# Low parts of the weights: all on VectorE while branch A is open, every second one on GpSimd elsewhere

## The chip, the cores and the metric

The kernel runs on one core of a Trainium2 chip. The metric is the device time of one execution in microseconds. TensorE (PE) multiplies matrices, VectorE (DVE), ScalarE (ACT) and GpSimd (POOL) work element by element, SyncE (SP) issues most of the transfers.

## What is computed

One step of a trunk of two layers, on 384 tokens (128 of a prompt, 256 of a latent grid) of width 2048. Each layer projects the modulated stream once, runs three mixers on the parts, and projects their outputs back:

```python
proj = jnp.matmul(u, lp['w_in']).astype(f32)
...
y_a, s_rwkv = rwkv_mixer(a_rkv, (a_wdf, a_wdb), (a_adf, a_adb), a_gate, lp, s_rwkv0)
y_b, mstate = mlstm_mixer(b_qk, b_v, b_o, b_i, b_f, b_gate, lp, mstate0)
y_c, kv_own = diff_attn_mixer(c_q, c_k, c_v, c_gate, lp, lam_init, ctx_kv)
mixed = jnp.concatenate([y_a, y_b, y_c], axis=-1).astype(x.dtype)
out = jnp.matmul(mixed, lp['w_out'])
x_new = layer_norm(DEEPNORM_ALPHA * x + gate[:, None] * out, lp['ln_g'], lp['ln_b'])
```

A is a recurrence with a 64x64 state per head in both directions, B a chunked matrix memory, C a differential attention.

## The kernel before

**Projections.** The two big projections are done in three products of fp32r numbers: the activations are kept as a high part `uh` and a low part `ul`, and so is each weight. A tile `raw` of weights comes by DMA in two halves of 128x512 (128x520 for B's values). `cut` splits a half: ScalarE copies it to `hi`, rounded to fp32r, and one subtraction, `raw - hi`, makes `lo`. A counter `ncut` gives every fourth subtraction to GpSimd (`CPOOL = 4`), the others to VectorE. There are four buffers each of `hi` and `lo`, and 688 halves in the program. PE then multiplies `uh,hi`, `ul,hi` and `uh,lo` into an `acc` tile: 12 matmuls for a usual half, 9024 in the program.

**The order.** One Python object, `Hybrid`, writes all instructions down in the order in which every engine will run them; each engine is a queue. The plan of a layer is a list of projection steps. The mixers are generators ("streams") that yield between short groups of instructions. Between projection steps `pump` lets streams go on whose inputs are ready by the planner's own clocks: `spend` adds to an engine's clock what `cost` says of an instruction, for VectorE 1.042 per element and 69, for GpSimd's two-input operations 2.1 per element and 149. `pump` returns when VectorE's or ScalarE's clock is more than `SLACK` ahead of PE's. Which engine gets a low part therefore goes into the order of everything behind it. No time on the chip goes into it.

**Branch A.** `a_start` spawns four streams: `AF` (`a_front`), `AD` (`a_blocks`), `AI` (`a_inverse`) and `A` (`a_scan`, with `a_end`). They pass 12 units (a chunk of 64 tokens in one direction) from one to the next; `AF` may be at most two units ahead of the scan. A unit's front begins with four `LP,lora` matmuls into a tile that becomes `th`; behind the last unit `AF` computes a bonus for each of four head pairs, with matmuls `big,const`. Branch A must be out of the tile `big0` before B's first projection is written there:

```python
def b_first(self):
    self.drain("AF")
    ...
    self.QK = self.mt([128, 8, T], "big0")
```

`drain` goes on with every stream that is ready, the one with the earliest clock first, until the named stream has ended; no projection step is written in that time. `b_first` stands in the plan ahead of B's first `q` step (`MIX`), behind 2304 projection matmuls of the program in layer 0 and 6816 in layer 1. A second `drain("A", "post")` follows at `to_b`, three steps later.

Of the kernel before, what the change touches and what calls it, by code (L numbers as in the profile page):

```python
# [14 lines left out]
AF = mybir.ActivationFunctionType  # L15
# [31 lines left out]
FILL = (4, 4, 4)  # L47
BLOCKS = (8, 4)
LAGP, LAGX = (100.0, 150.0), 0.0
CPOOL = 4  # L50
PESHARE = 2000.0, 2000.0
HEAD = ("PG", 2), ("QHt", 2), ("Tt", 2), ("BK", 1), ("QH", 1), ("UV", 1), ("ce00", 1), ("ce10", 1)
MIX = "cccqqqvvvvq", "cccqqqvvvvq"
# [148 lines left out]
class Hybrid:  # L202
# [212 lines left out]
    def execute(self, plan):  # L415
        data = [st for st in plan if st.kind != "c"]
        HB = KB // 2
        raws, halves = {}, {}
        issued = at = 0
        ring = RAWB + len(self.extra)  # L420
        early, taken, free = self.early, [], set()
        rooms = [i for i, st in enumerate(data) if st.room]

        def load(upto):
            nonlocal issued
            while issued < min(upto, len(data)):
                st, i = data[issued], issued
                if st.room:
                    k = rooms.index(i)
                    if k >= len(ROOMS) and rooms[k - len(ROOMS)] not in free:  # L430
                        return
                    tag, n, o = ROOMS[k % len(ROOMS)]
                    if o == 0:
                        self.room = self.mt([128, n], tag, bufs=2 if tag == "GE" else 1)
                    r = self.room[:, o:o + 1024]
                elif i < early and i % ring >= RAWB:
                    r = self.extra[i % ring - RAWB]
                elif len(taken) >= RAWB and taken[-RAWB] not in free:
                    return
                else:  # L440
                    taken.append(i)
                    r = self.keep("wp", self.wp.tile([128, KB * WMAX], F32, tag="raw", bufs=RAWB, name=self.nm("raw")), RAWB)
                k = st.parts * HB
                rv = r[:, 0:k * st.n].rearrange("p (k c) -> p k c", k=k)
                self.nc.sync.dma_start(rv, st.src())
                raws[i] = (r, rv, self.end)
                issued += 1

        def ahead(j):
            n = j + (ring if j < early else LOADS)  # L450
            load(n + sum(1 for i in rooms if j < i < n + len(ROOMS)))

        def cut(j, h):
            st = data[j]
            r, rv, t = raws[j]
            n = HB * st.n
            hi = self.keep("wp", self.wp.tile([128, HB * WMAX], F32R, tag="hi", bufs=CUTB, name=self.nm("hi")), CUTB)
            lo = self.keep("wp", self.wp.tile([128, HB * WMAX], F32R, tag="lo", bufs=CUTB, name=self.nm("lo")), CUTB)
            x = r[:, n * h:n * h + n]
            self.nc.scalar.copy(hi[:, 0:n], x)  # L460
            self.ncut = (self.ncut + 1) % CPOOL
            (self.nc.vector if self.ncut else self.nc.gpsimd).tensor_tensor(lo[:, 0:n], x, hi[:, 0:n].bitcast(F32), OP.subtract)
            if h == st.parts - 1:
                free.add(j)
            halves[j, h] = tuple(y[:, 0:n].rearrange("p (k c) -> p k c", k=HB) for y in (hi, lo)) + (self.end,)

        def front():

            k = (j, 1) if data[j].kind == "w" and now + 1 < data[j].parts else (j + 1, 0)
            if k in halves:  # L470
                return halves[k][2]
            return raws[k[0]][2] if k[0] in raws and data[k[0]].kind == "a" else 0.0

        self.more, self.front = lambda: cuts(j, now), front
        todo = [(j, h) for j, st in enumerate(data) if st.kind == "w" for h in range(st.parts)]

        def cuts(j, h):

            nonlocal at
            while at < len(todo) and todo[at] <= (j, h):  # L480
                cut(*todo[at])
                at += 1
            n = sum(1 for x in halves if x > (j, h))
            while at < len(todo) and n < CUTB - (1 if data[j].kind == "w" else 0) and todo[at][0] < issued:
                if raws[todo[at][0]][2] > self.clk["PE"] + AHEAD[self.l]:
                    break
                cut(*todo[at])
                at += 1
                n += 1
                ahead(j)  # L490

        j = now = self.ncut = 0
        ahead(0)
        for st in plan:
            if j == len(data):
                self.more, self.front = lambda: None, lambda: 0.0
            if st.kind == "c":
                st.fn()
                self.pump()
                continue  # L500
            ahead(j)
            if st.kind == "a":
                now = 1
                cuts(j, 1)
                r, rv, t = raws.pop(j)
                st.fn(rv)
            else:
                for h in range(st.parts):
                    now = h
                    cuts(j, h)  # L510
                    hv, lv, t = halves.pop((j, h))
                    st.fn(h, hv, lv)
                raws.pop(j)
            free.add(j)
            j, now = j + 1, 0
# [458 lines left out]
    def a_start(self):  # L974
        self.spawn(self.a_norm(), "N", lambda: self.have["k"] < 4)
        self.units, self.fronts, self.blocks = {}, {}, {}
        self.nf = self.nd = self.ni = self.ny = 0
        self.hold = False
        self.spawn(self.a_scan(), "A", lambda: self.have["v"] < 4 or (self.ny < 12 and self.ny >= self.ni))
        self.spawn(self.a_blocks(), "AD", lambda: self.nd < 12 and (self.nd >= self.nf or self.nd > self.ni))  # L980
        self.spawn(self.a_inverse(), "AI", lambda: self.ni < 12 and self.ni >= self.nd)
        self.spawn(self.a_front(), "AF", lambda: self.hold and self.nf - self.ny >= 2 or any(self.have[x] < n for x, n in (("n", 4), ("r", 4), ("lora", 2))))

    def a_lora(self, j, src):
        for d in range(2):
            o, i = self.LW[64 * j:64 * j + 64, d, :], src[64 * d:64 * d + 64]
            if j == 0:
                self.act(o, i, AF.Tanh)
            else:
                self.nc.scalar.copy(o, i)  # L990
        self.have["lora"] += 1
        yield
# [1100 lines left out]
```

## Time and profile before

| | before |
|---|---|
| median of 3 runs | 2233.82 us (2230.44 to 2238.89) |
| the profiled execution | 2234.41 us, of which the span 2232.7 us |
| PE busy | 2131.0 us, 95% |
| DVE busy | 1376.1 us, 62% |
| ACT busy | 950.1 us, 43% |
| POOL busy | 651.1 us, 29% |
| mean granted PE clock | 0.983 of full speed |

Busy time is the time in which an engine has at least one instruction under way. PE's matmuls overlap, so their own durations add up to more than its busy time, and one fp32 matmul can stand in the trace as two records. The line number of nearly all instructions is L155, the helper through which they are issued, so rows are told apart by their tiles: `mx` is a PSUM tile of the mixers, `acc` one of the projections, `mixed` holds A's working data (and the gates and outputs), `GE`, `QH`, `PG`, `Xo`, `Xd` and `th` are A's, `ce`, `cmx`, `cq` and `ck` are attention's.

### The profile page before, as it was taken

The numbers are of one execution on the slowest core, as the hardware profiler recorded it, in microseconds if no ns is written. First come the engines' busy times: TensorE is split into PE (matmuls) and PEld (weight loads), VectorE is DVE, ScalarE is ACT, GpSimd is POOL, SyncE is SP. The second block draws the span as 40 slices with busy tenths as digits, with TensorE's granted clock in tenths as the row PEclk, the third lists the DMA queues.
The fourth block names the chain that finished last, engine by engine and source line by source line (L and its number), as shares of the span: only waits on it lengthen the run. The fifth ranks groups of instructions, "written<-read, shape, count | busy, mean of one in ns | idle before, by whom it ended". The sixth has DMA issues, their size and how long they took to land. (4 is left out here: it accounts for less than half of the span.)

```text
span 2232.7 us, 44851 instructions
## 1 busy us (share of the span) xinstructions
PE 2131.0 (95%) x17261; PEld 1875.6 (84%) x17261; DVE 1376.1 (62%) x3704; ACT 950.1 (43%) x2215; POOL 651.1 (29%) x930
## 2 busy tenths in 40 slices
PE   6999999999999999999998999999999999999998
PEld 3778878778778788889997998787888789999997
DVE  2667766766675523578338677776776754367634
ACT  3345344353343533445326453444444354344543
POOL 3111433324332211111435223242343312111344
PEclk9999999999999999999998999999999999999998
DMA  9995433433434464554465442223232224333444
GB/s 323 317 320 148 135 112 110 128 100 108 148 99 137 151 194 155 171 154 152 153 198 185 137 123 91 78 76 105 70 93 79 78 83 152 114 114 118 141 146 144
DMA packets 313791, 314.83 MB, mean 141 GB/s; under 512 B 17569, under 2 KB 309030, under 8 KB 313450
## 3 DMA queue, kind: packets, MB, share of 16 engines
q1 hardware_dynamic: 305450, 299.49, 43.1%
q0 software_dynamic: 3616, 10.22, 1.4%
q8 instruction: 136, 2.23, 0.4%
q10 hardware_dynamic: 4512, 2.26, 0.4%
q14 instruction: 77, 0.63, 0.1%
HBM read 298.81 MB, written 13.12 MB: 140 GB/s over the span
## 5 line engine op out<-in xcount | busy, mean ns | idle before, releaser
L155 PE MATMUL acc<-uh,hi 128*128 128x384 f32 x2240 | 808.0, 361 | 11.6 <-ACT uh L155 7.7
L155 PE MATMUL acc<-uh,lo 128*128 128x384 f32 x2240 | 763.0, 341 | 5.8 <-POOL lo L155 3.4
L155 PE MATMUL acc<-ul,hi 128*128 128x384 f32 x2240 | 762.9, 341 | 1.3 <-DVE ul L155 1.3
L155 DVE TENSOR_TENSOR lo<-raw,hi 128x512 fp32r<-128x512 f32 (+1 forms) x496 | 361.8, 739 | 519.2 <-ACT hi L155 508.7
L155 ACT CAST hi<-raw 128x512 fp32r<-128x512 f32 (+1 forms) x659 | 395.7, 618 | 401.3 <-PE acc L155 259.4
L155 POOL TENSOR_TENSOR lo<-raw,hi 128x512 fp32r<-128x512 f32 (+1 forms) x163 | 221.9, 1361 | 927.3 <-ACT hi L155 860.0
L155 PEld LDWEIGHTS acc<-uh,hi 128*128 128x128 f32 x2240 | 426.6, 190 | 76.4 <-issue 35.8
L155 PEld LDWEIGHTS acc<-uh,lo 128*128 128x128 f32 x2240 | 425.3, 190 | 9.2 <-DVE lo L155 4.9
L155 PEld LDWEIGHTS acc<-ul,hi 128*128 128x128 f32 x2240 | 426.2, 190 | 6.0 <-DVE ul L155 3.1
L155 PE MATMUL acc<-hi,uh 128*128 128x256 f32 (+1 forms) x768 | 226.5, 295 | 2.8 <-ACT hi L155 1.1
L155 PE MATMUL acc<-lo,uh 128*128 128x256 f32 (+1 forms) x768 | 216.8, 282 | 1.0 <-DVE lo L155 1.0
L155 PE MATMUL acc<-hi,ul 128*128 128x256 f32 (+1 forms) x768 | 216.1, 281 | 0.0
L155 PEld LDWEIGHTS acc<-hi,uh 128*128 128x128 f32 x768 | 144.5, 188 | 20.3 <-issue 10.9
L155 PEld LDWEIGHTS acc<-lo,uh 128*128 128x128 f32 x768 | 144.6, 188 | 1.8 <-DVE lo L155 1.8
L155 PEld LDWEIGHTS acc<-hi,ul 128*128 128x128 f32 x768 | 144.7, 188 | 0.0
L155 ACT ACTIVATE ce<-mx,cmx 128x384 f32<-128x384 f32 (+1 forms) x96 | 48.0, 505 | 113.2 <-DVE cmx L155 110.1
L155 PE MATMUL ada<-raw,sil 128*32 128x256 f32 x1088 | 88.4, 399 | 1.8 <-DMA raw<-in_w_ada_dram 1.8
L155 ACT COPY mixed<-mx 64x256 f32<-64x256 f32 x120 | 44.0, 366 | 104.4 <-PE mx L155 102.7
L155 PEld LDWEIGHTS mx<-mixed 128*64 128x64 f32 x1536 | 53.5, 139 | 26.3 <-issue 11.1
L155 PE MATMUL mx<-mixed 128*64 128x64 f32 x1536 | 66.9, 230 | 3.3 <-DVE mixed L155 2.9
L155 DVE TENSOR_TENSOR mixed<-mx,mixed 128x256 f32<-128x256 f32 (+1 forms) x96 | 40.1, 418 | 30.1 <-PE mx L155 29.7
L155 DVE TENSOR_REDUCE cmx<-mx 128x1 f32<-128x384 f32 (+1 forms) x96 | 40.4, 460 | 19.8 <-PE mx L155 19.5
(435 smaller groups left out, 2940.5 us busy)
## 6 DMA issues: line engine op xcount, KB each, us to landing
raw<-in_w_in_dram SPq DMA_DIRECT2D x224, 512.0 KB
raw<-in_w_ada_dram SPq DMA_DIRECT2D x136, 512.0 KB
raw<-in_w_out_dram SPq DMA_DIRECT2D x64, 512.0 KB
big<-in_w_ada_dram SPq DMA_DIRECT2D x42, 512.0 KB
raw<-in_w_in_dram SPq DMA_DIRECT2D x32, 520.0 KB
GE<-in_w_ada_dram SPq DMA_DIRECT2D x14, 512.0 KB
cq<-xs SPq DMA_DIRECT2D x32, 192.0 KB
big<-in_w_in_dram SPq DMA_DIRECT2D x21, 256.0 KB
```

What stands on the lines that cost most here:

```text
L155: r = f(*args, **kw)
```

## The change

`CPOOL` becomes 2, and while one of A's four streams is open the counter is held at 1, which sends the low part to VectorE:

```diff
--- before.py
+++ after.py
@@ -47,7 +47,7 @@
 FILL = (4, 4, 4)
 BLOCKS = (8, 4)
 LAGP, LAGX = (100.0, 150.0), 0.0
-CPOOL = 4
+CPOOL = 2
 PESHARE = 2000.0, 2000.0
 HEAD = ("PG", 2), ("QHt", 2), ("Tt", 2), ("BK", 1), ("QH", 1), ("UV", 1), ("ce00", 1), ("ce10", 1)
 MIX = "cccqqqvvvvq", "cccqqqvvvvq"
@@ -458,7 +458,8 @@
             lo = self.keep("wp", self.wp.tile([128, HB * WMAX], F32R, tag="lo", bufs=CUTB, name=self.nm("lo")), CUTB)
             x = r[:, n * h:n * h + n]
             self.nc.scalar.copy(hi[:, 0:n], x)
-            self.ncut = (self.ncut + 1) % CPOOL
+
+            self.ncut = 1 if self.busy_a() else (self.ncut + 1) % CPOOL
             (self.nc.vector if self.ncut else self.nc.gpsimd).tensor_tensor(lo[:, 0:n], x, hi[:, 0:n].bitcast(F32), OP.subtract)
             if h == st.parts - 1:
                 free.add(j)
@@ -980,6 +981,9 @@
         self.spawn(self.a_blocks(), "AD", lambda: self.nd < 12 and (self.nd >= self.nf or self.nd > self.ni))
         self.spawn(self.a_inverse(), "AI", lambda: self.ni < 12 and self.ni >= self.nd)
         self.spawn(self.a_front(), "AF", lambda: self.hold and self.nf - self.ny >= 2 or any(self.have[x] < n for x, n in (("n", 4), ("r", 4), ("lora", 2))))
+
+    def busy_a(self):
+        return any(s.name in ("A", "AD", "AI", "AF") for s in self.streams)
 
     def a_lora(self, j, src):
         for d in range(2):
```

Of the 688 low parts GpSimd makes 172 in the program before and 189 in the changed one: while A is open 76 before and none now (36 and 40 in the two layers), elsewhere 96 before and 189 now. The instructions themselves, and those of PE, ACT and SP, are the same; their order changes where the planner's clocks lead to another choice.

On GpSimd, in layer 1 at the front of the twelfth and last unit of A (`GE`, `QH`, `ci` and `big` are its products, `th` a memset; `UV` and `Xd` belong to the scan and the inverse), there stands before:

```order
L155 COPY UV_20345<-big_2795_14457 64x256 x2
L155 TENSOR_TENSOR Xd_20159<-Xd_20159,own_20350 128x256
L155 MEMSET th_20381 128x4
L155 TENSOR_TENSOR lo_20398<-raw_20176,hi_20397 128x512
L155 TENSOR_TENSOR GE_20512<-th_20381,big_2793_14455 64x256
L155 TENSOR_TENSOR QH_20518<-q_3978_20384,BK_20377 64x4x2x64
L155 TENSOR_TENSOR ci_20521<-BK_20377,big_2793_14455 128x256
L155 TENSOR_TENSOR big_2793_14455<-ci_20521,Tt_14957 128x4x64
```

and in the changed program, at the same front:

```order
L155 COPY UV_20745<-big_2795_14457 64x256 x2
L155 TENSOR_TENSOR Xd_20548<-Xd_20548,own_20750 128x256
L155 TENSOR_TENSOR GE_20870<-th_20717,big_2793_14455 64x256
L155 TENSOR_TENSOR QH_20876<-q_4056_20720,BK_20713 64x4x2x64
L155 TENSOR_TENSOR ci_20879<-BK_20713,big_2793_14455 128x256
L155 TENSOR_TENSOR big_2793_14455<-ci_20879,Tt_15073 128x4x64
```

The subtraction `lo` is gone from between A's products; no other stands on GpSimd from A's opening to its end.

On PE, in layer 1, the bonus of A (`big,const`) stands before between projection matmuls, ahead of the place where `b_first` drains `AF`:

```order
L155 MATMUL mx_20691<-mixed_14454 64x64 x8
L155 MATMUL mx_20701<-big_2793_14455,const 128x384
L155 MATMUL acc_20654<-uh_125,hi_20531 128x384
L155 MATMUL acc_20654<-ul_126,hi_20531 128x384
L155 MATMUL acc_20654<-uh_125,lo_20532 128x384
L155 MATMUL acc_20655<-uh_125,hi_20531 128x384
L155 MATMUL acc_20655<-ul_126,hi_20531 128x384
L155 MATMUL acc_20655<-uh_125,lo_20532 128x384
L155 MATMUL mx_20710<-mixed_14454 64x64 x8
L155 MATMUL mx_20721<-big_2793_14455,const 128x384
L155 MATMUL mx_20724<-mixed_14454 64x64 x8
```

In the changed program the four bonus matmuls are the end of a row of instructions without any projection matmul (`cvc,ce` and `cvv,ce` are attention's), and the first matmul of the step behind `b_first` follows:

```order
L155 MATMUL mx_21009<-cvc_4023_20603,ce_4109_20913 128x128
L155 MATMUL mx_21009<-cvv_19762,ce_4109_20913 128x128 x2
L155 MATMUL mx_21015<-big_2793_14455,const 128x384
L155 MATMUL mx_21018<-mixed_14454 64x64 x8
L155 MATMUL mx_21067<-big_2793_14455,const 128x384
L155 MATMUL mx_21070<-mixed_14454 64x64 x8
L155 MATMUL mx_21081<-big_2793_14455,const 128x384
L155 MATMUL mx_21084<-mixed_14454 64x64 x8
L155 MATMUL mx_21107<-big_2793_14455,const 128x384
L155 MATMUL acc_21117<-uh_125,hi_20435 128x384
L155 MATMUL acc_21117<-ul_126,hi_20435 128x384
L155 MATMUL acc_21117<-uh_125,lo_20436 128x384
```

That row of instructions is what `drain("AF")` writes in layer 1. Before it wrote nothing there. It now holds 204 instructions on PE (170 matmuls and 34 transposes, 128 of them 64x64 matmuls), 109 on DVE (12 of them row maxima of attention, 7 shuffles), 57 on ACT and 43 on POOL, of A's units 10 to 12 and of the last two heads of C. The front of the twelfth unit begins in it:

```order
L155 MATMUL mx_20657<-LP_14459,lora_12739 128x128 x4
L155 MATMUL mx_20665<-const,ce_4029_20615 128x128
L155 MATMUL mx_20668<-mixed_14454 64x64 x8
L155 MATMUL mx_20678<-cvv_19762,ce_4020_20594 128x128
L155 MATMUL mx_20686<-cvv_19762,ce_4030_20617 128x128
L155 MATMUL mx_20690<-mixed_14454 64x64 x8
```

Before, that front stood 162 projection matmuls ahead of `b_first`. In layer 0 both programs have `AF` ended ahead of `b_first`; the drain writes nothing.

## Rows read from the trace of the kernel before

**Rows 1.** Page, part 1: busy time and share of each engine.

```profile
span 2232.7 us, 44851 instructions
PE 2131.0 (95%) x17261; PEld 1875.6 (84%) x17261; DVE 1376.1 (62%) x3704; ACT 950.1 (43%) x2215; POOL 651.1 (29%) x930
```

**Rows 2.** Windows, four stretches: busy us (records) by engine, clock, DMA.

```profile
core 0: us, PE busy (x) PEld busy (x) DVE busy (x) ACT busy (x) POOL busy (x), PEclk, DMA share, GB/s
230.00:760.00 530.00, 505.66 (x4949) 419.81 (x4947) 355.56 (x1054) 221.21 (x597) 169.31 (x279) 0.98 0.40 120
760.00:1290.00 530.00, 513.18 (x3360) 471.51 (x3353) 290.24 (x720) 223.22 (x464) 142.04 (x166) 0.99 0.53 165
1290.00:1790.00 500.00, 474.02 (x4653) 414.82 (x4652) 362.77 (x1029) 215.19 (x567) 175.78 (x283) 0.99 0.30 88
1790.00:2232.00 442.00, 429.88 (x2744) 406.78 (x2744) 236.32 (x610) 196.44 (x411) 116.35 (x133) 0.98 0.40 127
```

**Rows 3.** PE's waits (us, times, longest): 1290 to 1790 us, then 230 to 760.

```profile
PE mx L155 <- DVE mixed L155: 7.3, 7, 3.2
PE mx L155 <- DVE GE L155: 3.6, 5, 1.4
...
PE mx L155 <- DVE ce L155: 2.2, 2, 2.1
PE mx L155 <- DVE csm L155: 1.8, 1, 1.8
...
PE acc L155 <- DVE VC L155: 0.8, 1, 0.8
...
PE mx L155 <- DVE mixed L155: 6.8, 5, 2.7
PE mx L155 <- DVE GE L155: 3.6, 6, 1.5
...
PE mx L155 <- DVE mod L155: 3.2, 2, 1.7
...
PE acc L155 <- DVE lo L155: 1.5, 2, 1.2
```

**Rows 4.** Groups by shape (busy us, mean ns, idle before): low parts, whole span.

```profile
L155 DVE TENSOR_TENSOR lo<-raw,hi 128x512 fp32r<-128x512 f32 x448 | 329.0, 744 | 419.5 <-ACT hi L155 409.0 <-PE acc L155 5.4 <-PE mx L155 2.7
...
L155 POOL TENSOR_TENSOR lo<-raw,hi 128x512 fp32r<-128x512 f32 x147 | 201.0, 1367 | 791.2 <-ACT hi L155 723.8 <-PE mx L155 37.4 <-PE acc L155 10.9
```

**Rows 5.** Out-projection of layer 1: window, then GpSimd's sums (groups).

```profile
2100.00:2200.00 100.00, 100.00 (x572) 100.00 (x571) 36.88 (x64) 42.95 (x75) 46.76 (x40) 1.00 0.51 165
...
L155 POOL TENSOR_TENSOR ce<-ce,gt 128x384 f32<-128x384 f32 x26 | 37.3, 1436 | 0.3 <-ACT gt L155 0.3
...
L155 POOL TENSOR_TENSOR ce<-ce,mixed 128x384 f32<-128x384 f32 x26 | 26.4, 1016 | 0.1
```

**Rows 6.** Timeline of PE: start us, us, instructions, xcount.

```profile
1727.02 0.61 PE L155 MATMUL mx<-LP,lora 128*128 128x128 f32 x4
...
1767.00 0.81 PE L155 MATMUL mx<-big,const 128*128 128x384 f32 x2
...
1783.23 0.45 PE L155 MATMUL acc<-uh,hi 128*128 128x384 f32 x1
1783.51 0.34 PE L155 MATMUL acc<-ul,hi 128*128 128x384 f32 x1
1783.69 0.34 PE L155 MATMUL acc<-uh,lo 128*128 128x384 f32 x1
1783.87 0.34 PE L155 MATMUL acc<-uh,hi 128*128 128x384 f32 x1
```

**Rows 7.** Windows of one tile: mx, then lo in two stretches.

```profile
core 0: us, PE busy (x) PEld busy (x) DVE busy (x) ACT busy (x), PEclk, DMA share, GB/s
1290.00:1790.00 500.00, 175.41 (x2775) 136.68 (x2776) 86.36 (x208) 82.57 (x255) 0.99 0.30 88
...
core 0: us, PE busy (x) PEld busy (x) DVE busy (x) POOL busy (x), PEclk, DMA share, GB/s
1290.00:1790.00 500.00, 190.31 (x594) 112.49 (x594) 74.76 (x99) 45.85 (x33) 0.99 0.30 88
...
1790.00:2232.00 442.00, 236.08 (x730) 137.13 (x730) 87.41 (x123) 56.60 (x41) 0.98 0.40 127
```

**Rows 8.** Groups: attention's row maxima, LP,lora matmuls, activation of th.

```profile
L155 DVE TENSOR_REDUCE cmx<-mx 128x1 f32<-128x384 f32 (+1 forms) x96 | 40.4, 460 | 19.8 <-PE mx L155 19.5
...
L155 PE MATMUL mx<-LP,lora 128*128 128x128 f32 x192 | 26.6, 281 | 0.8 <-DVE GE L155 0.8
...
L155 ACT ACTIVATE th<-th 128x512 f32<-128x512 f32 x24 | 15.2, 632 | 54.4 <-DVE th L155 54.4
```

**Rows 9.** Windows at the layer boundary, columns as in rows 2.

```profile
1183.00:1193.00 10.00, 6.45 (x20) 5.53 (x21) 9.57 (x17) 6.59 (x14) 6.65 (x10) 0.53 0.51 172
1193.00:1204.00 11.00, 11.00 (x64) 10.74 (x63) 8.96 (x15) 9.50 (x21) 6.88 (x8) 1.00 0.44 145
```

**Rows 10.** Timeline: a low part on GpSimd and one on VectorE.

```profile
1344.87 1.30 POOL L155 TENSOR_TENSOR lo<-raw,hi 128x512 fp32r<-128x512 f32 x1 [1.18 <-ACT hi L155]
...
1345.35 1.37 DVE L155 TENSOR_TENSOR lo<-raw,hi 128x512 fp32r<-128x512 f32 x1 [1.88 <-ACT hi L155]
```

## The prediction

> **What bounds the kernel now.** I read the page first: of the span TensorE (PE) is busy 95%, VectorE (DVE) 62%, GpSimd (POOL) 29% [rows 1]. So the time is TensorE's work plus its idle time, 102 us, and an engine that only gets more or less busy changes nothing until TensorE waits for it. Then the stretches [rows 2]: branch A is open at about 230 to 760 us and 1290 to 1790 us, and there TensorE is idle for 24.3 and 26.0 us, with VectorE at 67% and 73%. In the other two stretches it is idle 16.8 and 12.1 us, much of that at the layer boundary and the end. Third, TensorE's waits in the two A stretches [rows 3]: small ones, mostly for branch A's own VectorE results (`mixed`, `GE`); for low parts little (VectorE's 1.5 us in layer 0, and none above 1 us in layer 1). So low parts are not what TensorE waits for. What they do is take time from an engine on which branch A's chain runs.
>
> **Low parts by themselves.** A low part takes 744 ns on VectorE and 1367 ns on GpSimd [rows 4]. In the order of the changed kernel the low parts of GpSimd go from 172 to 189, of 688: in the two A stretches from 76 to 0, elsewhere from 96 to 189. So VectorE gets 76 more in A, 57 us of work, 40 of them (30 us) in layer 1, and GpSimd 93 more elsewhere, 127 us. Elsewhere they are covered: in the out-projection (2100 to 2200 us) TensorE has no idle time with GpSimd at 47% [rows 5]; a second low part per four adds some 16 us there, GpSimd is then at 63%, and a low part that queues behind two of its sums (1.44 and 1.02 us [rows 5]) is ready 3.8 us after its high part. The four buffers of halves give about three halves of matmuls, 12 each at some 0.175 us (the spacing of starts in [rows 6]), 6.3 us. If that cover fails, or the last sums ahead of the layer's statistics stand behind one more low part, it costs one low part per layer, 2 x 1.37 us. I take +1 (0 to +3).
>
> **The order of layer 1.** The planner charges VectorE for the moved low parts, so it lets branch A's steps out later. In layer 0 the order hardly moves: A's front is through before `b_first` in both kernels. In layer 1 it is not. Before, the front of the last unit (its `LP,lora` matmuls) stands at 1727.0 us, the last bonus matmul (`big,const`) at 1767.0, and the first matmul after `b_first` (projection matmul 6817 of 9024 in the order) at 1783.2 [rows 6]: `drain("AF")` finds nothing to do, with 16 us to spare, 40 us after the front began. In the changed kernel that front has not even begun when `b_first` is reached. The drain then runs front, inverse, scan and the attention steps that are ready, one after another, with no projection matmul between: 204 instructions on PE, 109 on DVE, 57 on ACT, 43 on POOL, the list in the section on the change.
>
> How long is that? VectorE's records in 1290 to 1790 us without low parts are 288.0 us over 930 [rows 2, 7], 0.310 each; 109 instructions and the seven mask loads of the shuffles make 35.9. Twelve of them are attention row maxima at 0.460 instead [rows 8]: +1.8. In three places all streams hang on a short chain through PE and ACT (`LP,lora` 0.61 and `th` 0.63 us; the scores of the long blocks; the last bonus, 0.81 for a pair of records) [rows 6, 8]: I estimate 2 us each from these, +6. Together 44 us at full TensorE clock. TensorE's own work in it: an fp32 matmul leaves two records (192 for `LP,lora` [rows 8], of 96 instructions in the order), so 170 matmuls and 34 transposes are 374 records at 0.0632 us (175.41 over 2775 [rows 7]), 23.6 us. At half clock that would be 47 us, and with the chains 54 for the stretch. The clock does fall where VectorE has the work and TensorE waits: in 1183 to 1193 us, with PE busy 6.45 of 10 us and DVE 9.57, the granted clock is 0.53, close to the lower level of 1.2 GHz, and it is back at 1.00, 2.4 GHz, in the next 11 us [rows 9]. A drain with TensorE about half busy is nearest to that row, so I take 48, between 44 and 54. The 23.6 us are work that before lay between projection matmuls and has to be done anyway, so the drain adds 48 - 23.6 = **+24.4** (ends: 36 - 23.6 = +12 and 54 - 23.6 = +30). Behind it the clock has to come back: +2 (0 to +5, the 4.7 us that 0.53 over 10 us costs).
>
> What comes back: the steps that sit in the drain no longer interrupt the projection. Their share of A's idle time is 374 of 2775 records of 26.0 us: -3.5 (0 to -3.5).
>
> **One shared resource.** At 1344.87 us GpSimd starts a low part of 1.30 us, and VectorE's own low part, started at 1345.35, takes 1.37 us instead of the mean 0.74 [rows 4, 10]; it ends 0.55 us after GpSimd's. So a GpSimd low part can hold VectorE up. But over the 99 low parts of VectorE in 1290 to 1790 us the mean is 0.755 (74.76 over 99), against 0.711 in 1790 to 2232 (87.41 over 123) [rows 7]: a few per cent. From these I take -2 for what A gains. The Trainium skill (SBUF — State Buffer, section SBUF: two separate sides) says that the two engines share a port pair that is locked for a whole instruction, a VectorE instruction with two SBUF inputs against a GpSimd one, and that the loser blocks. The pair at 1345 us agrees. By that rule each GpSimd low part taken out of A could give VectorE back its full length; by it the sum would be that of the second rival, which is priced below from rows.
>
> Sum: 24.4 + 2 - 3.5 - 2 + 1 = +21.9 on the profiled execution's 2234.4 us, which is within 0.1% of the median 2233.8: **2256 us**. I call anything within 0.5% (11 us) no change; the three runs before differ by 0.4%.
>
> **Rivals.**
> 1. *The drain, mostly paid back: no change.* If the drain runs at its lower end (+12), because its streams interleave well and the clock holds, and A's steps cause the usual fewer waits (-3.5), the time is some 2243. For it: six streams are ready in the drain. Against it: VectorE alone has 36 us of instructions there. Its place is `b_first` of layer 1; below a drain of 35 us it decides.
> 2. *Relief of VectorE: faster.* If each of the 76 GpSimd low parts in A held VectorE for its full 1.37 us, 104 us of VectorE's time come free, A's results are there before TensorE asks, and the waits for them vanish (15.7 us in the five VectorE rows of layer 1, 15.1 in the four of layer 0 [rows 3]: -31), and with them the low clock of layer 0's stretch (0.98 over 530 us [rows 2]: -11). Without the relief term my sum is +23.9; 23.9 - 31 - 11 = -18, 2216 us. It turns the sign where relief exceeds 24 us and shows as faster beyond 35. Against it: the means of the low parts above, and that the order, drain included, is fixed in the program: a quicker VectorE doesn't dissolve it.
> 3. *Worse:* the drain at half clock throughout (+30), 5 us to come back, 3 elsewhere, no relief: 2272 or a little over.
>
> **Chances and range.** The forecast case, 2245 to 2272: 0.74. Rival 1: 0.15. Rival 2: 0.06. Rival 3 beyond 2272: 0.05. Faster by over 0.5%: 0.06; within: 0.15; slower: 0.79. The range for 8 in 10 runs from 2242 (drain +12, all of the give-back) to 2272.
>
> **What would show it.** In the profile after: one stretch late in layer 1's A, 40 to 55 us long, without `acc` matmuls, with DVE at 70% or more, PE at about half and the clock below 1; PE's idle time there about 20 to 30 us and waits for `mixed`, `GE`, `ce` and `big` in it. In layer 0 the idle time should stay within some 8 us of 24.3, POOL busy in A should fall by 87 us in all (45.85 in layer 1 [rows 7]), and TensorE should still have no idle time in the out-projections. I am wrong if that stretch is under 35 us, if its loss is won back by fewer waits in both A stretches, or if TensorE begins to wait for GpSimd's low parts in the heads or out-projections.

## The result, and the profile after

The changed kernel takes 2255.1 us (median of 5 runs, 2245.61 to 2256.24) against 2233.8 before in the same comparison: ratio **1.0084** (of the means), 95% interval 1.0055 to 1.0113, slower by 12 to 25 us. The forecast was 2256 (2242 to 2272) and slower. The total is right; the three terms that make it up are not, and that they cancel is luck, as the experiments show. The profiled execution took 2255.25 us.

Page, part 1, and the row of the mean granted TensorE clock, of the changed kernel; they answer to [rows 1]:

```profile
span 2253.5 us, 44909 instructions
PE 2139.0 (95%) x17261; PEld 1880.5 (83%) x17261; DVE 1359.9 (60%) x3687; ACT 951.7 (42%) x2215; POOL 672.7 (30%) x947
...
die 0 (median of its cores): 2253.5 us, clock 0.978
```

TensorE's idle time went from 101.7 to 114.5 us (+12.8) and its busy time, for the same 17261 records, by +8.0. The lower clock is enough to explain the longer busy time: 1 - 0.978 of 2253.5 us is 49.6 us lost, against 38.0 before (0.983). So a stall can be paid as idle time and again as slow work behind it; the section on the hardware comes back to that.

The four stretches of the changed kernel (columns as in [rows 2]; the times are the same, the work in them is not quite):

```profile
230.00:760.00 530.00, 510.70 (x5032) 425.96 (x5031) 368.98 (x1109) 231.97 (x620) 143.58 (x280) 1.00 0.41 126
760.00:1290.00 530.00, 505.86 (x3260) 462.80 (x3259) 274.71 (x650) 214.89 (x442) 192.46 (x181) 0.98 0.51 159
1290.00:1790.00 500.00, 468.12 (x4392) 409.85 (x4392) 357.82 (x1028) 215.52 (x575) 128.47 (x242) 0.96 0.29 89
1790.00:2232.00 442.00, 435.31 (x2955) 410.90 (x2951) 216.55 (x582) 189.65 (x390) 139.74 (x160) 0.98 0.38 119
```

Layer 0's A stretch improved: idle 19.3 us in place of 24.3, clock 1.00 in place of 0.98. The stretch behind it, where A is closed, got worse: idle 24.1 in place of 16.8, with GpSimd at 192 us in place of 142. Layer 1's A stretch lost most: idle 31.9 and clock 0.96, in place of 26.0 and 0.99.

The drain of layer 1 is there as forecast, with no projection matmul in it. PE's timeline of the changed kernel (columns as in [rows 6]): the front of the last unit, the last bonus, the first matmul behind `b_first`.

```profile
1753.53 2.05 PE L155 MATMUL mx<-LP,lora 128*128 128x128 f32 x8 [0.19 <-ACT mixed L155]
...
1802.16 0.91 PE L155 MATMUL mx<-big,const 128*128 128x384 f32 x2
1802.62 0.63 PE L155 MATMUL acc<-uh,hi 128*128 128x384 f32 x1
```

The last projection matmul ahead of it starts at 1740.4, so the stretch without projection matmuls is 62.2 us long. Windows of the changed kernel over the whole of it, and over the drain alone (columns as in [rows 2]):

```profile
1740.50:1802.60 62.10, 47.62 (x418) 34.67 (x417) 39.94 (x128) 26.47 (x84) 14.29 (x26) 0.67 0.10 31
1744.30:1802.60 58.30, 44.30 (x374) 32.51 (x375) 36.14 (x119) 23.37 (x75) 10.76 (x22) 0.65 0.10 33
```

Of PE's 418 records two are ends of projection matmuls, and the next 42, up to 1744.3 us, were written ahead of `b_first` (8 of them `ada`). The drain itself is the 374 records of the forecast, and it takes 58.3 us; the forecast had 48, between 44 and 54. VectorE has 36.1 us of work in it, close to the 37.7 that were estimated without the chains. But the clock is 0.65 (a mean between full speed, 2.4 GHz, and half, 1.2 GHz, so some 41 of the 58 us at half), and PE is busy for 44.3 us. In the chain of work that ended last, PE's `mx` matmuls are 59.0% of these 58.3 us, 34 us: PE and VectorE work by turns. The largest of PE's waits within the stretch (1740.4 to 1802.6; us, times, longest) are for attention's `ce` and A's `GE` and `UV`, with 0.5 us for `mixed` and 0.2 for `big`:

```profile
PE mx L155 <- ACT ce L155: 9.8, 5, 5.5
PE mx L155 <- DVE GE L155: 1.9, 3, 0.7
PE mx L155 <- ACT UV L155: 1.5, 1, 1.5
```

Low parts: the groups of the changed kernel that answer to [rows 4], then the tile `lo` by stretches (columns as in [rows 7]).

```profile
L155 DVE TENSOR_TENSOR lo<-raw,hi 128x512 fp32r<-128x512 f32 x452 | 348.3, 782 | 370.3 <-ACT hi L155 366.9 <-PE acc L155 2.7
L155 POOL TENSOR_TENSOR lo<-raw,hi 128x512 fp32r<-128x512 f32 x143 | 193.1, 1351 | 456.5 <-ACT hi L155 438.4 <-PE acc L155 6.5 <-DMA big<-in_w_ada_dram 5.9
```

```profile
760.00:1290.00 530.00, 276.32 (x841) 159.28 (x841) 99.91 (x101) 128.01 (x93) 0.98 0.51 159
1290.00:1790.00 500.00, 187.54 (x587) 110.61 (x586) 97.80 (x132) 0.00 (x0) 0.96 0.29 89
1790.00:2232.00 442.00, 238.86 (x736) 138.83 (x736) 72.73 (x94) 92.15 (x70) 0.98 0.38 119
```

Here is the surprise. In 760 to 1290 us VectorE makes 101 low parts at 0.989 us each; in the last stretch 94 at 0.774, against 0.711 before [rows 7]. A low part next to GpSimd's is not 0.74 us any more, and VectorE's mean rises. The first of these stretches in the kernel before:

```profile
760.00:1290.00 530.00, 281.60 (x860) 162.29 (x861) 108.56 (x150) 68.76 (x50) 0.99 0.53 165
```

And some of GpSimd's come late. PE's waits for them over the whole execution, before and changed:

```profile
PE acc L155 <- POOL lo L155: 3.4, 2, 2.6
PE acc L155 <- POOL lo L155: 9.0, 8, 3.7
```

7.3 of the 9.0 us lie in 691 to 945 us, around and behind the close of A in layer 0. The longest one, in the timeline (ScalarE's high parts, GpSimd, then PE):

```profile
750.32 1.14 ACT L155 CAST hi<-raw 128x512 fp32r<-128x512 f32 x2 [3.00 <-DMA raw<-in_w_in_dram]
751.79 1.13 ACT L155 CAST hi<-raw 128x512 fp32r<-128x512 f32 x2
...
751.56 0.68 POOL L155 TENSOR_TENSOR crs<-crs,css 128x3 f32<-128x3 f32 x1
752.32 0.38 POOL L155 TENSOR_SCALAR crs<-crs 128x3 f32<-128x3 f32 x1
752.79 0.19 POOL L155 TENSOR_TENSOR crs<-crs 128x3 f32<-128x3 f32 x1
753.09 1.50 POOL L155 TENSOR_SCALAR cq<-cq,crs 128x128 f32<-128x128 f32 x3
754.55 2.49 POOL L155 TENSOR_TENSOR lo<-raw,hi 128x512 fp32r<-128x512 f32 x2
...
755.87 0.67 PE L155 MATMUL acc<-uh,lo 128*128 128x384 f32 x1 [3.71 <-POOL lo L155]
```

The high parts are there by 752.9; GpSimd is still in attention's `crs` and `cq`, and only then makes two low parts in a row. TensorE waits 3.71 us. In the out-projection of layer 1, where the forecast looked for cover, there is cover (window of the changed kernel, columns as in [rows 5]): no idle time with GpSimd at 59%.

```profile
2122.00:2222.00 100.00, 100.00 (x571) 100.00 (x571) 29.72 (x52) 42.61 (x75) 59.08 (x52) 1.00 0.50 163
```

### The profile page after: what moved, and what is told of

Its sections match the earlier page's. It is cut to its first block, busy times and chain, and to the rows that moved or that the text cites. A ratio compares the mean times of both kernels' runs of the same rounds, so it can differ in the third digit from the quotient of the medians.

```text
span 2253.5 us, 44909 instructions
## 1 busy us (share of the span) xinstructions
PE 2139.0 (95%) x17261; PEld 1880.5 (83%) x17261; DVE 1359.9 (60%) x3687; ACT 951.7 (42%) x2215; POOL 672.7 (30%) x947
## 4 chain that ended last, share of the span: by engine, by line
PE 72%; DVE 15%; DMA 6%; ACT 5%; issue 2%; POOL 1%; SPq 0%; DVEq 0%; ACTq 0%; POOLq 0%
PE acc L155 52%; PE mx L155 17%; DMA raw<-in_w_in_dram 4%; DVE lo L155 4%; PE ada L155 3%; ACT hi L155 2%; DVE GE L155 1%; DVE mixed L155 1%; DVE cmx L155 1%; DVE big L155 1%; ACT ce L155 1%; DMA cr<-in_cache_attn_k_dram 1%; DVE dn L155 1%; DVE brs L155 1%; DVE tm L155 0%
## 5 line engine op out<-in xcount | busy, mean ns | idle before, releaser
L155 DVE TENSOR_TENSOR lo<-raw,hi 128x512 fp32r<-128x512 f32 (+1 forms) x486 | 384.6, 802 | 481.3 <-ACT hi L155 477.9
L155 POOL TENSOR_TENSOR lo<-raw,hi 128x512 fp32r<-128x512 f32 (+1 forms) x173 | 233.0, 1347 | 628.6 <-ACT hi L155 610.6
L155 POOL TENSOR_TENSOR Xo<-Xo,Xd 128x256 f32<-128x256 f32 x24 | 19.2, 798 | 166.1 <-DVE Xd L155 135.1
```

The costliest lines, as they stand in the source:

```text
L155: r = f(*args, **kw)
```

## The experiments

The change does two things: it gives low parts to other engines, and, since the planner charges them, it puts instructions in another order. The first theory is the forecast's: the order, with its drain, costs some 23 us, the rest nearly nothing. The rival: the engines matter too, with the sign by place. The first four kernels take order and engines apart. A second counter decides which engine really makes a low part, while `ncut` still tells the planner; on every engine the instructions, low parts apart, stand exactly as in the kernel whose order is named. Diffs are against the changed kernel and are cut to the lines that matter (the reset of a new counter and the tile `dup` are left out); "before" was 2240.0 us in this comparison, 2237.7 and 2237.5 in the two later ones, so ratios are compared.

**Order of before, A's low parts on VectorE, elsewhere every fourth on GpSimd.**

```diff
-            self.ncut = 1 if self.busy_a() else (self.ncut + 1) % CPOOL
-            (self.nc.vector if self.ncut else self.nc.gpsimd).tensor_tensor(lo[:, 0:n], x, hi[:, 0:n].bitcast(F32), OP.subtract)
+            self.ncut = (self.ncut + 1) % 4
+            self.rcut = 1 if self.busy_a() else (self.rcut + 1) % 4
+            args = lo[:, 0:n], x, hi[:, 0:n].bitcast(F32)
+            (self.nc.vector if self.rcut else self.nc.gpsimd)._e.tensor_tensor(*args, OP.subtract)
+            self.spend("DVE" if self.ncut else "POOL", "tensor_tensor", args[0], args[1:], [])
```

> The order of the kernel before, instruction for instruction on every queue; only the low parts made while branch A is open go to VectorE (76 of them). Elsewhere GpSimd keeps every fourth. Theory 1 (GpSimd's low parts hold up A's VectorE chain, and that is what the two A stretches won): 20 to 37 us less than before, 2197 to 2214. Theory 2 (the A stretches won because the new order puts A's steps elsewhere): within 8 us of 2234. My prediction's own term was -2 us.

Measured: 2231.07 us, ratio 0.9963 (0.9948 to 0.9978), -8.3 us. That is just beyond the second theory's 8 us (the interval is 5 to 12) and far from the first's 20: A's relief is real, four times the 2 us of the forecast, and a fifth of what the second rival needed (31 + 11). But the late low parts behind A's close are there already, with every fourth elsewhere; PE's waits for GpSimd's low parts over the whole execution:

```profile
PE acc L155 <- POOL lo L465: 8.0, 7, 4.6
```

All seven lie between 768 and 948 us.

**Order of before, A as before, elsewhere every second on GpSimd.** As above, but:

```diff
+            self.rcut = (self.rcut + 1) % (4 if self.busy_a() else 2)
```

> The order of the kernel before; in A every fourth low part stays on GpSimd, elsewhere GpSimd makes every second (93 more). Theory 1 (more low parts on GpSimd cost time outside A, by low parts that come late and by VectorE held up): 15 to 30 us more than before, 2249 to 2264. Theory 2 (the time lost behind A in the changed kernel is due to its order): within 8 us of 2234. The prediction's term was +1 us.

Measured: 2252.91 us, ratio 1.0058 (1.0038 to 1.0077), +13.0 us (9 to 17), near the first theory's lower end. The term that the forecast had at +1, with an upper end of +3, is the larger of the two engine terms. Late low parts are few in this kernel:

```profile
PE acc L155 <- POOL lo L465: 6.9, 2, 4.5
```

They stand where before has its two, near 770 and 1850 us. The profiled execution took 2243.0 us against the median of 2252.9, so its trace holds only a part of the 13 us.

**Order of before, the engines of the changed kernel.**

```diff
+            self.rcut = 1 if self.busy_a() else (self.rcut + 1) % 2
```

> The order of the kernel before, but each low part on the engine that the changed rule gives it: all on VectorE in A, every second on GpSimd elsewhere. There is no drain at b_first of layer 1. If the two parts add up, it is before plus what the two single runs show, some 2225 (2215 to 2240). If the drain is the whole of the loss, it is well below the changed kernel's 2255, by 15 us or more. If the drain cost nothing, 2255.

Measured: 2243.73 us, ratio 1.0016 (1.0000 to 1.0031), +3.6 us. The two parts alone give 0.9963 x 1.0058 = 1.0021: they add up (the 2225 expected was a guess at the two single results, and missed). Against the changed kernel it is 1.0084 / 1.0016, 0.68% or 15 us less: the new order, which has the drain, is most of the loss.

**Order of the changed kernel, the engines of before.**

```diff
-            self.ncut = 1 if self.busy_a() else (self.ncut + 1) % CPOOL
+            self.ncut = 1 if self.busy_a() else (self.ncut + 1) % 2
+            self.rcut = (self.rcut + 1) % 4
```

> The order of the changed kernel, with its drain of 204 PE instructions at b_first of layer 1, but GpSimd makes every fourth low part everywhere, as before. If the order, through the drain, is what costs: 30 to 45 us more than before, 2264 to 2279, and the stretch without projection matmuls is about 62 us again. If the drain is paid back by denser work around it: 2234 to 2245.

Measured: 2253.04 us, ratio 1.0060 (1.0040 to 1.0080), +13.4 us, between the two expectations, with the stretch of the drain 61.4 us long. So the account is: order +13.4, A's relief -8.3, elsewhere +13.0, together +18.1; measured 0.84%, 18.8 us.

**What does a low part on GpSimd cost where A is closed?** First the order of before with no low part on GpSimd at all:

```diff
+            self.rcut = 1
```

> The order of before on PE, ACT and SP; all 688 low parts on VectorE, none on GpSimd. Before, VectorE has 516 and GpSimd 172 (76 while A is open, 96 elsewhere). Theory 1: a GpSimd low part costs something wherever it stands (it comes late, or holds VectorE up), at about the same price each: the 76 in A were worth 8.3 us, 93 more elsewhere cost 13.0 us, so taking away all 172 gives -8.3 and 96 x 0.14 = -13.4, ratio 0.990 (0.987 to 0.993), about 2218 us. Theory 2: elsewhere the first GpSimd low part in four is covered and only the second one in four costs; then the time is that of the first experiment, ratio 0.996. Theory 3: VectorE, with about 71 us more work than before elsewhere, comes late itself in the heads and out-projections; ratio 1.000 or more.

Measured: 2214.24 us, ratio 0.9894 (0.9879 to 0.9908): the first theory's 0.990. VectorE makes all 688 and is not late; PE's waits for its low parts are 1.8 us in all. So a GpSimd low part costs, net of what it saves VectorE, about 24 us / 172 = 0.14 us, also where A is closed and at one in four.

How little it saves VectorE stands in part 1 of the pages. The kernel with A's low parts moved, then this one:

```profile
PE 2138.0 (96%) x17261; PEld 1879.3 (84%) x17261; DVE 1388.7 (62%) x3781; ACT 950.4 (43%) x2215; POOL 550.5 (25%) x853
PE 2118.9 (96%) x17261; PEld 1864.1 (84%) x17261; DVE 1417.3 (64%) x3876; ACT 950.5 (43%) x2215; POOL 428.2 (19%) x758
```

Against the 1376.1 us of [rows 1] VectorE makes 77 and 172 low parts more, and is busy for only 12.6 and 41.2 us more, where 0.69 us each would be 53 and 119. The rest came back from its other instructions: the same 3188 of them take 1123.1 us before, 1082.4 and 1065.0 in these two kernels, summed over the traces' records.

Three ways remain in which a GpSimd low part can cost: its result is late, GpSimd's own other work is late behind it, or it takes VectorE's time. The next two kernels take this one and let GpSimd repeat the subtraction from the same inputs into a bfloat16 tile `dup` that nothing reads; PE, ACT, SP and DVE keep their order.

```diff
+            self.nc.vector._e.tensor_tensor(*args, OP.subtract)
+            self.dcut = (self.dcut + 1) % 4 if self.busy_a() else 1
+            if not self.dcut:
+                self.nc.gpsimd._e.tensor_tensor(self.dup[:, 0:n], *args[1:], OP.subtract)
```

> The kernel with the order of before and all low parts on VectorE (ratio 0.9894), to which GpSimd, while branch A is open, repeats every fourth subtraction raw - hi from the same inputs at the same place (77 in all) into a tile that nothing reads; its output is bfloat16. Theory 1 (a GpSimd low part costs because its result comes late to TensorE): nobody waits for these, ratio 0.988 to 0.991. Theory 2 (it costs because GpSimd's instruction takes VectorE's time, or GpSimd's own work for A comes late behind it): the 8 us that A's relief was worth are lost again, ratio 0.993 or more, with VectorE's mean time in A longer.

Measured: 2260.16 us, ratio 1.0099 (1.0076 to 1.0121): 46 us above the kernel without them, 0.60 us for each of the 77. With the repeats where A is closed:

```diff
+            self.dcut = 1 if self.busy_a() else (self.dcut + 1) % 2
```

> The same with the repeated subtractions where A is closed, every second one (190 in all), none in A. Theory 1 (lateness of the result): ratio 0.988 to 0.991, though GpSimd is as busy as in the changed kernel. Theory 2 (shared time): the price found so far is about 0.14 us for each GpSimd low part there, so 190 x 0.14 = 26 us come back, ratio about 1.001; between the two, both count.

Measured: 2280.72 us, ratio 1.0190 (1.0168 to 1.0212): +66 us, 0.35 us for each of the 190. No one waits for these results as data, so lateness of the result alone is out; GpSimd's instruction hurts by running. That GpSimd's other work is late is a small part at most with the repeats elsewhere: PE's waits for it are 1.8 us without them and 1.9 with them, ScalarE's waits for GpSimd none and 10.8. With the repeats in A (PE's 5.4 us) this way is not excluded. What grows most is VectorE's time. With the repeats elsewhere its 3876 instructions, the same as without, keep it busy for 1529.1 us, 111.8 more:

```profile
PE 2151.3 (94%) x17261; PEld 1882.3 (83%) x17261; DVE 1529.1 (67%) x3876; ACT 949.0 (42%) x2215; POOL 746.9 (33%) x948
```

`lo` in two stretches, first without repeats, then with them where A is closed (VectorE's is the last busy time):

```profile
760.00:1290.00 530.00, 285.55 (x873) 164.25 (x872) 141.12 (x204) 0.99 0.54 165
1790.00:2232.00 442.00, 231.22 (x716) 134.50 (x716) 113.75 (x160) 0.98 0.40 124
```

```profile
760.00:1290.00 530.00, 265.27 (x802) 152.85 (x801) 178.74 (x187) 0.97 0.52 157
1790.00:2232.00 442.00, 231.23 (x714) 134.77 (x715) 132.87 (x163) 0.98 0.39 116
```

VectorE's own low part goes from 0.692 us to 0.956 in the first stretch, for the same instruction. The longest of PE's waits of the kernel with the repeats name mostly VectorE's results:

```profile
PE mx L155 <- DVE big L155: 16.3, 16, 2.0
PE acc L155 <- DVE ul L155: 12.0, 5, 5.5
PE acc L155 <- ACT hi L155: 11.6, 12, 1.9
```

without repeats `big` is 6.8 us, `ul` 3.1, `hi` 6.3. The sizes went beyond the second theory's 8 and 26 us. Two things in these kernels add to them: VectorE still makes its own, and both start at the same high part, so they meet by construction; and transfers of the next weights wait for the repeats to leave `raw` (SP's queue, 56.8 us over 30 waits with the repeats in A, 69.3 over 49 elsewhere). The prices are upper bounds, then, and not those of a low part that GpSimd makes in VectorE's place.

**What does the drain cost?** The changed kernel with a planner that lets A go on:

```diff
-SLACK = 2200.0, 2500.0
+SLACK = 2200.0, 3000.0
```

> The changed kernel with the planner's slack of layer 1 raised from 2500 to 3000, so that it lets A's steps out earlier and drain(AF) of layer 1 writes nothing; the engines of the low parts by the changed kernel's rule. Theory 1 (the drain is what the new order costs): the 13 us of the order come back, 2241 to 2246 us, ratio to before 1.000 to 1.004, no stretch over 10 us without acc matmuls in 1700 to 1810 us. Theory 2 (the order costs by its other differences, or A's steps then wait as long between projection matmuls): ratio 1.007 or more.

Measured: 2233.69 us, ratio 0.9987 (0.9973 to 1.0002). The drain writes nothing, and around its place TensorE is nearly always busy (window of this kernel, columns as in [rows 2]):

```profile
1690.00:1810.00 120.00, 118.30 (x1185) 100.61 (x1186) 84.08 (x258) 54.25 (x149) 30.07 (x60) 0.99 0.29 85
```

Against the changed kernel that is 1.0084 / 0.9987, 0.97% or 21.7 us: more than the 13 of the first theory, and the second's 1.007 is out. It is the price of the drain and not of the drain alone, since TensorE's order differs from the changed kernel's from 1311 us on, the beginning of layer 1's A. And with the same engines the order without a drain is better than before's: 0.9987 / 1.0016, -6.5 us (with intervals that just touch). So the order's +13.4 hides a drain of nearly 22 us and, by difference, a gain elsewhere of 6 to 8.

Is that gain the slack? The kernel before with that one number changed in the same way:

> The kernel before with the planner's slack of layer 1 at 3000 in place of 2500, nothing else. The kernel with all of A's low parts on VectorE and this slack ran at 0.9882, with the order of before at 0.9963. Theory 1: the slack is what made that order better by some 18 us; then this runs at 0.992 (0.990 to 0.995). Theory 2: the order is better since the planner was told of the low parts; the slack alone is worth nothing, 0.999 to 1.002.

Measured: 2243.14 us, ratio 1.0022 (1.0007 to 1.0036): at the second theory's upper edge. The slack alone gains nothing, so what is left is that the planner knows of VectorE's work. In the kernel without a drain A's twelve fronts of layer 1 stand 0 to 36 projection matmuls later than before; which of the moved steps brings the gain was not tested.

Why was the drain 58 us long and not 48? The changed kernel, with fillers on PE in the drain:

```diff
             self.segment(min(can, key=lambda s: s.t))
+            if names == ("AF",):
+                warm = warm or self.acc()
+                self.nc.tensor._e.matmul(warm[:, 0:128], self.ident, self.ident, start=True, stop=True)
```

> The changed kernel with 42 additional fp32 128x128 matmuls (ident by ident, into an acc tile that the next projection overwrites), one behind each segment of drain(AF) in layer 1, some 9 us of PE work at full clock; nothing else is changed. Theory 1: the drain is 62 us long and not 48 because the clock falls to half in it and PE's steps lie on the chain; with PE busier the clock stays higher, the drain falls to about 50 us and the time by some 10 us, to 2245. Theory 2: the drain's length is VectorE's work and chains; the clock hardly matters; the drain stays at 60 to 63 us and the time within 2 us of the changed kernel's 2255. Theory 3: the additional matmuls lie on the chain themselves: 66 to 72 us, and the time some 5 to 9 us longer.

(The fillers are 66 matmuls, 132 records; 42 was miscounted.) Measured: 2265.45 us, ratio 1.0120 (1.0106 to 1.0134), some 8 us above the changed kernel. The window of the stretch in this kernel:

```profile
1749.90:1816.40 66.50, 58.84 (x549) 46.70 (x549) 41.57 (x132) 26.45 (x84) 16.95 (x36) 0.85 0.10 30
```

The clock rose from 0.67 to 0.85, and 11 us more of PE work took only 4.4 us more of the stretch; but it did not get shorter. That is the third theory's result: PE's steps lie on the chain. In this trace the fillers themselves are 26.7% of the chain that ended last in these 66.5 us, and PE's other matmuls 41.5%. How much of the drain's 58 us the low clock alone makes stays open.

**Without the drain and without the second half.** A's low parts on VectorE, the planner told, elsewhere one in four:

```diff
-CPOOL = 2
+CPOOL = 4
-SLACK = 2200.0, 2500.0
+SLACK = 2200.0, 3000.0
```

> The rule of the change for branch A alone (all low parts on VectorE while A is open), CPOOL at 4 elsewhere, and the planner told so, with layer 1's slack at 3000 so that drain(AF) writes nothing. Theory 1 (relief in A is worth 8 us and the order costs only by its drain): ratio 0.996 (0.993 to 0.998), about 2231 us. Theory 2 (any order other than that of before costs some us, by waits between projection matmuls): ratio 1.000 to 1.005.

Measured: 2208.18 us, ratio 0.9882 (0.9862 to 0.9901), better than either theory, and 18 us better than the same engines in the order of before. PE's waits in 1290 to 1790 us of this kernel, against the first part of [rows 3]:

```profile
PE mx L155 <- DVE GE L155: 4.0, 3, 1.4
PE mx L155 <- DVE mixed L155: 3.7, 2, 3.0
PE mx L155 <- ACT ce L155: 2.2, 4, 1.4
```

`mixed` went from 7.3 us in 7 waits to 3.7 in 2. Last, all low parts on VectorE with the planner told:

```diff
-            self.ncut = 1 if self.busy_a() else (self.ncut + 1) % CPOOL
+            self.ncut = 1
-SLACK = 2200.0, 2500.0
+SLACK = 2200.0, 3000.0
```

> All 688 low parts on VectorE, the planner told so, slack of layer 1 at 3000 (drain(AF) writes nothing). Theory 1: the gains add up: 0.9882 with A's low parts on VectorE and this slack, less another 13 us for the 96 elsewhere, ratio 0.982 (0.979 to 0.985), about 2197 us. Theory 2: with a better order the late low parts elsewhere were hidden, or VectorE comes late: 0.987 or more.

Measured: 2207.27 us, ratio 0.9861 (0.9843 to 0.9880). The fastest version here, 1.4% below before, but no better than the one above by what can be told (0.2%, with intervals that overlap). That lies between the theories, at the second's edge of 0.987: the gains do not add up in full. PE's waits for VectorE's low parts are 1.7 us, so VectorE is not late; that the better order covers most of GpSimd's one low part in four would fit, and was not shown.

## Why the prediction was right, and which terms were not

1. **Place and kind of the loss: right.** `drain(AF)` of layer 1 is one stretch without projection matmuls, it is the largest single loss that was found, and without it the time falls by 21.7 us. The forecast's net for it was 24.4 + 2 - 3.5 = +22.9.
2. **"The drain adds 48 - 23.6": mis-sized.** The drain takes 58.3 us, beyond the upper end of 54, so the term is 58.3 - 23.6 = +34.7. Its 374 records of PE were right, and VectorE's work was (36.1 us for 37.7). What failed is the path: the forecast let VectorE's work set the length and put PE's work on the chain in three places only, while PE's matmuls are 59.0% of the chain. The sentence "A drain with TensorE about half busy is nearest to that row" failed with it: PE was busy for 76% of the drain at clock 0.65 and idle for 14.0 us (forecast 20 to 30), VectorE for 62% (forecast 70% or more). That the kernel without a drain is only 21.7 us faster may mean that those steps are not free between projection matmuls either; that was not measured. (Two slips in the working: 47 + 6 is 53 and not 54, and the lower end is 44 in one sentence and 36 in the next. The sum does not hang on them.)
3. **"What comes back: -3.5": too small.** Order against order, with the engines held, gives +13.4 to +15 (1.0060; 1.0084 / 1.0016), the kernel without a drain -21.7: by difference 6 to 8 us come back. "In layer 0 the order hardly moves" is not so either: idle time there is 19.3 us, predicted within 8 of 24.3, and PE's wait for `mixed`, 6.8 us in [rows 3], is gone from the view. Of that the engines and the order each make a part; the same wait in 230 to 760 us with A's low parts moved alone, then with the new order alone:

```profile
PE mx L155 <- DVE mixed L155: 2.8, 3, 1.6
PE mx L155 <- DVE mixed L155: 3.1, 3, 2.1
```

4. **"I take -2 for what A gains": -8.3.** The step that failed is reading A's price from the mean of VectorE's low parts (0.755 against 0.711). The price is mostly in VectorE's other instructions: with A's low parts moved they take 40.7 us less in all, and the "57 us of work" that the move was to give VectorE kept it busy for only 12.6 us more.
5. **"I take +1 (0 to +3)" for elsewhere: +13.0.** The cover was worked out in the out-projection, and there it holds (100.00 of 100 us in layer 1). But the forecast had the shared time of the two engines only in A; it works wherever both subtract. In 760 to 1290 us VectorE makes 101 low parts in place of 150, at 0.989 us each in place of 0.724: 49 fewer, and only 8.7 us saved. The prediction's own sign of being wrong, that TensorE begins to wait for GpSimd's low parts, did appear (9.0 us for 3.4, behind attention's `crs` and `cq` on GpSimd's queue), but these waits come with A's rule: 8.0 us with A's low parts moved alone. The half elsewhere alone has 6.9 us of them, 3.5 more than before. What the rest of the 13 us consists of was not measured.
6. **GpSimd in A:** 345.1 us in the two stretches before, 272.1 after, -73 of the forecast's -87. Its low parts there went from 87.4 to 5.1 us, as forecast but for four behind A's close in layer 0; the rest is other work of GpSimd that now falls into these windows.
7. **The sum:** -6.3 in A and +12 elsewhere offset an order term that was 9 us too high, so 2256 stood against 2255 with the wrong parts in it. That is luck, and no proof of the terms. The second rival's mechanism exists at a fifth of its price; the first rival's give-back was real, too, at twice the -3.5.

## What to carry to other kernels

To give every second one of a stream of elementwise operations to a slower engine relieves the faster one by less than the operation takes, when the two hold each other up: compare the first engine's busy time, over all of its instructions, with and without the other's operation before counting on relief. A change of engines in a kernel whose order comes from a planner is two changes; run each engine choice with the old order, and the new order with the old engines. And look for cover at the places where the helper's queue is full of other work, not in the stage that is the easiest to work out.

## What the runs showed of the hardware

**Two lengths of one instruction.** VectorE's 128x512 subtraction takes 0.69 us or, beside GpSimd's, up to 1.8. The clearest pair in the changed kernel, from its timeline:

```profile
1013.97 1.29 POOL L155 TENSOR_TENSOR lo<-raw,hi 128x512 fp32r<-128x512 f32 x1 [1.28 <-ACT hi L155]
1014.01 1.79 DVE L155 TENSOR_TENSOR lo<-raw,hi 128x512 fp32r<-128x512 f32 x1
```

VectorE starts 0.04 us after GpSimd and ends 0.54 us after it. Counted over the records of the traces, VectorE's low parts from `raw` (128x512 and 128x520) of over 1.2 us are 21 of 496 before, 69 of 486 in the changed kernel, 19 of 659 with all on VectorE and 86 of 659 with the repeats elsewhere; none of these ran without a GpSimd instruction under way, and those without one have a mean of 0.69 us. This agrees with the rule that the prediction cited from the Trainium skill (SBUF — State Buffer, section SBUF: two separate sides), that one of the two engines blocks for the other's whole instruction. The second rival, built on it, had a relief of 31 + 11 = 42 us in A; measured were 8.3. One thing that it left out shows in VectorE's busy time: the moved low parts gave back 40.7 us of its other work, but brought it 77 low parts more to make, so that it was busy for 12.6 us longer and not less.

**A wait can be paid a second time, by the clock.** The 3.71 us wait that ends at 755.87 nearly fills the first of these windows of the changed kernel; TensorE is busy for 0.29 us of it, and the clock is still 0.99. Behind it TensorE is busy throughout at a granted clock of 0.58, near the lower level of 1.2 GHz, and 4 us later at 1.00, 2.4 GHz:

```profile
752.00:756.00 4.00, 0.29 (x2) 0.14 (x1) 1.35 (x3) 0.93 (x2) 3.73 (x8) 0.99 0.41 131
756.00:760.00 4.00, 4.00 (x15) 4.00 (x16) 0.00 (x0) 0.56 (x1) 1.04 (x1) 0.58 0.66 198
760.00:764.00 4.00, 4.00 (x24) 4.00 (x23) 0.69 (x1) 0.68 (x2) 1.28 (x1) 1.00 0.23 72
```

Over whole executions the same shows in a sum. Loss by the clock is (1 - granted clock) x span:

| kernel | span | PE busy | PE idle | lost by the clock | busy less that |
|---|---|---|---|---|---|
| before | 2232.7 | 2131.0 | 101.7 | 38.0 | 2093 |
| changed | 2253.5 | 2139.0 | 114.5 | 49.6 | 2089 |
| all on VectorE, order of before | 2214.4 | 2118.9 | 95.5 | 19.9 | 2099 |
| the same with repeats elsewhere | 2279.0 | 2151.3 | 127.7 | 50.1 | 2101 |
| A on VectorE, planner told | 2205.4 | 2120.5 | 84.9 | 30.9 | 2090 |

By this estimate TensorE's work at full clock is the same within 12 us in all of them; between 2205 and 2279 us of span, idle time accounts for 43 us and the clock for 19, and the other 12 stay open. The two parts do not go together in every pair: the last kernel of the table has 10.6 us less idle time than the third and loses 11 us more by the clock. A forecast from idle time alone misses that second part.
